# Other PSUM banks, earlier weight forms and an earlier silu table for the first up group, and another order of the last sums and scalings, in a hybrid encoder block

## The chip, the cores and the metric

The kernel runs on one core of a Trainium2 chip. The metric is the device time of one execution in microseconds (us). The core has five engines that work side by side: TensorE (PE in the profile; PEld is its weight load), VectorE (DVE), ScalarE (ACT), GpSimd (POOL) and SyncE (SP). Each runs its own instructions in the order in which they stand in the program and waits on semaphores for the others. SP, ACT and POOL also issue DMAs. Matmul results go to PSUM, which this kernel uses as eight banks of 128x512 floats.

## What is computed

One encoder layer over 512 tokens of width 2048: a gated mixer of two attentions, then a SwiGLU feed-forward, and a final RMS norm. What bears on the change:

```python
h2 = rms_norm(x, norm2_w[l]) * (1.0 + sc2) + sh2
ff = (jax.nn.silu(h2 @ w_ffn_gate[l]) * (h2 @ w_ffn_up[l])) @ w_ffn_down[l]
x = x + g2 * ff
...
return rms_norm(x, final_w)
```

The gate and up matrices are 2048 x 5632, the down matrix is 5632 x 2048, all float32.

## The kernel before, in words

**Split products.** Every float32 operand is split into a high part (rounded, written by ACT) and a low part (source minus high part, by DVE): `split`, lines 134 to 136. A product is three matmuls (`mm3`, lines 142 to 145): high by high, high by low, low by high. Of weights, the line-143 and line-144 matmuls read the high part and the line-145 matmul the low part.

**Seven products.** Most feed-forward products are 2x2 block products done with seven block products in place of eight (`group7`, lines 916 to 944), numbered r = 1 to 7 and run in the order `ORDER` = 1, 2, 3, 5, 6, 7, 4. The weights of one such product are made by `wforms` (lines 870 to 890) from two 512 KB loads `raw`: r = 1 takes a block of the first load as it is, r = 2 and 3 take the second load, r = 5 and 6 take the sums `ta`, r = 7 and 4 take the sums `tb`. Each of these four is split into a buffer `whl`, of which there are five in turn; `raw` also has five in turn, `ta` two, `tb` one. The token side has forms of its own: `xsums` makes sums `sa` and `sb`, `xforms` splits them into `x56`, `x3` and parts of the tiles `m`. The second call of `xsums` for the last quarter takes its `sb` out of the one `tb` buffer, the other call takes two `raw` buffers.

**The gate and up loop.** There are 11 column groups of 512 (`for n in range(FU)`, line 1008), each with a gate and an up product over four quarters `s` of the 2048 features, in the order 2, 3, 0, 1. One quarter of one product is 7 x 12 = 84 matmuls. The very first gate group is done classically, without the seven products, by `first_products` (lines 958 to 967), because it runs while the normed and transposed tokens are only arriving (`h2_part`, lines 804 to 814, which uses the banks S, S, T in turn). It holds the four banks `mm` to its end. Then four silu activations (line 1015) empty these banks, and the first up group starts through `group7`. Its results go to banks after the table `BANK` (line 845): r = 1, 2, 3, 5 to the four `mm` banks, 6 and 7 to the two S banks, 4 to Y. The bank T takes four dummy transposes (`stirred`, line 847) after the first quarter of the first up group. At the end of a group (lines 935 to 944) ACT and DVE add the banks up, and the next group takes the banks by the same table.

**The order of instructions.** A scheduler orders each engine's instructions from the program's order, the dependences and priorities; `tc.high_priority()` moves what stands in it forward, and `behind` (`keep_in_program_order`, line 285) keeps an instruction in its place.

**The end.** The last stage (lines 1285 to 1315) goes over four blocks of 128 tokens, `i` = 0 to 3. For each of four column groups `cc` PE does 12 matmuls, DVE multiplies the bank by the gate (`ro`, line 1280) and adds the residual (line 1281; the tiles are `xa` for columns 0 and 1, `xb`, `xd`), and ACT sums the squares (line 1282). For blocks 0 to 2, `row_rstd` then makes the reciprocal root (`rr`), four DVE instructions scale the block (line 1301) and four stores leave, half from SP and half from ACT. For block 3 the columns are multiplied by the final weights ahead of the root (line 1296), which only has to wait for the square; the root's sums stand in a high-priority part (lines 1305 to 1309), and then one column group is scaled by ACT and three by DVE; SP issues three of the four stores.

Of the kernel before, what the change touches and what calls it, by code (L numbers as in the profile page):

```python
# [32 lines left out]
EPS = 1e-6  # L33
# [56 lines left out]
def encoder_block(ctx: ExitStack, tc, xp, xT, c, ada1_w, ada2_w, b_ada, norm1_w, w_in, q_norm_w, k_norm_w, bias,  # L90
                  w_oa, w_ob, w_out, norm2_w, w_gate, w_up, w_down, final_w, rope, out):
    nc = tc.nc
    V, S, G = nc.vector, nc.scalar, nc.gpsimd

    const = ctx.enter_context(tc.tile_pool(name="const", bufs=1))
    small = ctx.enter_context(tc.tile_pool(name="small", bufs=4))
# [27 lines left out]
    def bank(tag):  # L124
        return ps.tile([P, 512], F32, tag=tag, name=tag, bufs={"mm": 4, "S": 2, "T": 1, "Y": 1}[tag])
# [120 lines left out]
    def row_rstd(acc):  # L246
        ssq = small.tile([P, 1], F32, tag="ssq", name="ssq")
        V.reduce_sum(ssq, acc, axis=AX.X)
        return rsqrt_mean(ssq, D, 1)
# [190 lines left out]
    r = token_rstd()  # L440
# [363 lines left out]
    def h2_part(s, a, t):  # L804
        tp = bank(next(turn))
        for q in range(2):
            for c in range(2):
                o = (2 * q + c) * P
                nc.tensor.transpose(tp[:, o:o + P], xn[s][:, 2 * t + c, (2 * a + q) * P:(2 * a + q + 1) * P], ident)
        for q in range(2):  # L810
            k = 4 * s + 2 * a + q
            S.activation(feature(s, a, t)[:, q], tp[:, q * 256:(q + 1) * 256].rearrange("p (c n) -> p c n", c=2),
                         AF.Identity, scale=s2[:, k:k + 1], bias=t2[:, k:k + 1])
        split(*(quarter(h, t) for h in mx[2 * s + a]), feature(s, a, t))
# [28 lines left out]
    LATE = (1, 5, 6, 7, 4, 2, 3)  # L843
    HALVES = (1,), (2, 3), (5, 6), (7, 4)
    BANK = {1: "mm", 2: "mm", 3: "mm", 5: "mm", 6: "S", 7: "S", 4: "Y"}

    def stirred(b):

        for o in range(0, 4 * P, P):
            last = behind(nc.tensor.transpose(b[:, o:o + P], ident, ident))  # L850
        stir_last.append(last.ins)
# [61 lines left out]
        d[3] = tuple(blk(h, 0) for h in x3)  # L913
        return d

    def group7(wsrc, xs, order, dst, stir=False):

        bk = {r: bank(BANK[r]) for r in ORDER}
        for n, s in enumerate(order):
            w = wsrc(s)  # L920
            if stir and n == 1:
                tp = bank("T")
                stirred(tp)
            for r in ORDER:
                (wh, wl), (xh, xl) = w[r], xs[s][r]
                for q in range(2):
                    for c in range(2):
                        o = bk[r][:, c * 256:(c + 1) * 256]
                        cs = slice(c * P, (c + 1) * P)
                        first, last = n == 0 and q == 0 and c == 0, n == len(order) - 1 and q == 1  # L930
                        with after_stir():
                            mm3(o, wh[:, q, cs], wl[:, q, cs], xh[:, q], xl[:, q], first, last, skip_group_check=True)
        p = {r: b.rearrange("p (c n) -> p c n", c=2) for r, b in bk.items()}
        (d11, d12), (d21, d22) = dst
        with tc.high_priority():
            p1 = io.tile([P, 512], F32, tag="io", name="p1").rearrange("p (c n) -> p c n", c=2)
            S.activation(p1, p[1], AF.Copy)
            V.tensor_add(d11, p[2], p1)
            V.tensor_add(d21, p[6], p1)
            V.tensor_add(d12, p[5], d21)  # L940
            V.tensor_add(d12, p[3], d12)
            V.tensor_add(d21, p[7], d21)
            V.tensor_add(d22, p[5], d21)
            V.tensor_sub(d21, d21, p[4])
# [31 lines left out]
    for s in (2, 3, 0, 1):  # L976
        for e in range(2):
            first_products(s, e, 1, False, (s, e) == (1, 1))
            if parts:
                h2_part(*parts.pop(0), 1)  # L980
        if s not in f_x:
            sums = {0: xsums(0, raw_tile("sa"), raw_tile("sb")), 1: xsums(1)}
            p_r.release()
            ca = form_pool("ca", "right")
            f_x.update({n: form_pool(f"f{n}", "right") for n in (0, 1)})
            c_p = form_pool("c", "right")
        hx[s] = xforms(f_x[s], s, *(sums[s] if s < 2 else xsums(s)))
# [20 lines left out]
    for n in range(FU):  # L1008
        cs = []
        for w in (w_gate, w_up):  # L1010
# [8 lines left out]
            def wsrc(s):  # L1019
                d = wforms(w, 4 * s, n * 512)  # L1020
                if s == 1 and n == FU - 1 and w is w_up:
                    first_pairs()
                return d
# [258 lines left out]
        S.activation(io.tile([P, 512], F32, tag="io", name="junk")[:, :n], to, AF.Square, accum_out=acc)  # L1282

    last_sq = small.tile([P, 2], F32, tag="ssq", name="last_sq")
    for i in range(NT):
        sl = slice(i * P, (i + 1) * P)
        for cc in range(4):
            final = i == NT - 1 and cc == 3
            for h in range(1 + final):
                b = bank("mm" if (i or cc > 1) and not h else "S")  # L1290
                hs = slice(h * 256, h * 256 + 256) if final else slice(0, 512)
                for k in range(4):
                    mm3(b[:, hs], xs[k][0][:, sl], xs[k][1][:, sl], *(t[:, hs] for t in wl[cc][k]), k == 0, k == 3)
                column(i, cc, b, hs.start, hs.stop - hs.start, last_sq[:, 0:1] if final and h else sq3[i][:, cc:cc + 1])
                if i == NT - 1:
                    V.tensor_mul(x2[cc][:, i, hs], x2[cc][:, i, hs], fw[:, cc * 512 + hs.start:cc * 512 + hs.stop])
        if i < NT - 1:
            r = row_rstd(sq3[i])
            for cc in range(4):
                cs = slice(cc * 512, (cc + 1) * 512)  # L1300
                V.scalar_tensor_tensor(x2[cc][:, i], x2[cc][:, i], r, fw[:, cs], op0=ALU.mult, op1=ALU.mult)
                (nc.scalar if cc % 2 else nc.sync).dma_start(out[i * P:(i + 1) * P, cs], x2[cc][:, i])
            continue
        with tc.high_priority():
            V.reduce_sum(last_sq[:, 1:2], sq3[i], axis=AX.X)
            V.tensor_scalar(last_sq[:, 1:2], last_sq[:, 1:2], 1.0 / D, EPS, op0=ALU.mult, op1=ALU.add)
            ms = small.tile([P, 24], F32, tag="ms", name="ms")[:, :1]
            V.scalar_tensor_tensor(ms, last_sq[:, 0:1], 1.0 / D, last_sq[:, 1:2], op0=ALU.mult, op1=ALU.add)
            r = inverse_root(ms)
        for cc in (1, 3, 0, 2):  # L1310
            if cc == 1:
                S.activation(x2[cc][:, i], x2[cc][:, i], AF.Copy, scale=r)
            else:
                V.tensor_scalar(x2[cc][:, i], x2[cc][:, i], r, None, op0=ALU.mult)
            (nc.scalar if cc == 1 else nc.sync).dma_start(out[i * P:(i + 1) * P, cc * 512:(cc + 1) * 512], x2[cc][:, i])
    p_s.release()
    p_e.release()
    wq.release()
# [27 lines left out]
```

## Time and profile before

| what | us |
|---|---|
| median of 3 runs | 2565.15 |
| lowest and highest of these | 2564.49 and 2567.37 |
| the profiled execution: its own time | 2564.97 |
| the profiled execution: its span, from the first to the last instruction | 2563.2 |
| PE busy in that span | 2525.6 |
| DVE, ACT busy | 1880.0, 1021.3 |

All times below are counted from the start of the profiled span. The first up group stands at about 1293 us, the last stage begins near 2508 us. A timeline row gives start, duration, engine, line, operation, output and inputs, their sizes, and in brackets how long the engine was idle before it and what ended that. The 1.8 us between span and own time lie outside the first and last instruction.

### The profile page before, as it was taken

How to read it: one execution, taken by the hardware profiler on the slowest of the kernel's cores; microseconds unless marked ns; L12 is line 12 of the kernel's file. 1: busy time of each engine (PE TensorE's matmuls, PEld its weight loads, DVE VectorE, ACT ScalarE, POOL GpSimd, SP SyncE). 2: the span in 40 equal slices, each digit the busy share in tenths (PEclk: the TensorE clock that was granted, in tenths of full speed). 3: DMA queues.
4: the chain of work that ended last, by engine and by line, in shares of the span. 5: the costliest groups of instructions: out<-in, count | busy, mean ns of one | idle time of the engine just before them, and what ended most of it. 6: DMA issues, size and time to landing. Idle time of an engine off the chain costs nothing.

```text
span 2563.2 us, 40435 instructions
## 1 busy us (share of the span) xinstructions
PE 2525.6 (99%) x16525; PEld 2281.8 (89%) x16525; DVE 1880.0 (73%) x2499; ACT 1021.3 (40%) x1407; POOL 151.3 (6%) x254
## 2 busy tenths in 40 slices
PE   7999999999999999999999999999999999999997
PEld 5888788888888788888999999999999998999996
DVE  8984776456566567555798888888888885687877
ACT  5223544223333332225754444444444454434333
POOL 0000000111011111011000000000000000000010
PEclk8999999999999999999999999999999999999999
DMA  9864234855655877676444444433444456546562
GB/s 342 309 237 146 69 99 145 257 183 180 187 172 188 294 239 247 205 266 211 132 132 130 128 125 132 129 119 116 132 124 124 132 171 219 199 139 235 185 253 106
DMA packets 217466, 457.46 MB, mean 178 GB/s; under 512 B 15056, under 2 KB 68672, under 8 KB 208832
## 3 DMA queue, kind: packets, MB, share of 16 engines
q1 hardware_dynamic: 179872, 308.19, 37.5%
q0 software_dynamic: 29728, 132.20, 15.1%
q10 hardware_dynamic: 7680, 14.48, 1.6%
q8 instruction: 130, 2.13, 0.3%
q14 instruction: 56, 0.46, 0.1%
HBM read 410.74 MB, written 44.07 MB: 177 GB/s over the span
## 4 chain that ended last, share of the span: by engine, by line
PE 91%; DVE 4%; DMA 2%; ACT 1%; issue 1%; SPq 0%; DVEq 0%; ACTq 0%
PE mm L145 19%; PE mm L144 19%; PE mm L143 19%; PE S L143 7%; PE S L145 7%; PE S L144 7%; PE Y L143 3%; PE Y L144 3%; PE Y L145 3%; PE T L145 1%; PE T L144 1%; PE T L143 1%; DMA yr<-y 1%; DMA raw<-in_w_down 1%; DVE raw L414 1%
## 5 line engine op out<-in xcount | busy, mean ns | idle before, releaser
L135 ACT ACTIVATE whl<-raw 128x1024 fp32r<-128x1024 f32 (+1 forms) x483 | 464.3, 962 | 836.4 <-PE mm L145 381.5
L136 DVE TENSOR_TENSOR whl<-raw,whl 128x1024 fp32r<-128x1024 f32 (+1 forms) x483 | 531.6, 1110 | 315.9 <-ACT whl L135 315.4
L136 DVE TENSOR_TENSOR whl<-ta,whl 128x1024 fp32r<-128x1024 f32 x104 | 127.4, 1225 | 74.4 <-ACT whl L135 73.0
L135 ACT ACTIVATE whl<-tb 128x1024 fp32r<-128x1024 f32 x104 | 110.8, 1065 | 153.0 <-PE S L145 129.0
L135 ACT ACTIVATE whl<-ta 128x1024 fp32r<-128x1024 f32 x104 | 110.4, 1062 | 149.0 <-PE mm L145 104.7
L313 DVE SCALAR_TENSOR_TENSOR acc<-mw,cact,acc 128x1024 f32<-128x1024 f32 x124 | 158.5, 1278 | 14.0 <-DMA mw<-in_ada_w 13.8
L136 DVE TENSOR_TENSOR whl<-tb,whl 128x1024 fp32r<-128x1024 f32 x104 | 127.1, 1223 | 9.0 <-ACT whl L135 6.0
L291 POOL DMA_DIRECT2D mw<-in_ada_w x112 | 59.8, 534 | 713.6 <-DVE acc L313 422.0
L143 PE MATMUL S<-x56h,whl 128*128 128x256 f32 x336 | 92.8, 276 | 0.4 <-ACT whl L135 0.4
L144 PE MATMUL S<-x56l,whl 128*128 128x256 f32 x336 | 92.7, 276 | 0.0
L143 PE MATMUL mm<-x3h,whl 128*128 128x256 f32 x336 | 92.7, 276 | 0.0
L144 PE MATMUL mm<-x3l,whl 128*128 128x256 f32 x336 | 92.7, 276 | 0.0
L145 PE MATMUL mm<-x3h,whl 128*128 128x256 f32 x336 | 92.7, 276 | 0.0
L143 PE MATMUL mm<-x56h,whl 128*128 128x256 f32 x336 | 92.7, 276 | 0.0
L144 PE MATMUL mm<-x56l,whl 128*128 128x256 f32 x336 | 92.7, 276 | 0.0
L145 PE MATMUL mm<-x56h,whl 128*128 128x256 f32 x336 | 92.7, 276 | 0.0
L145 PE MATMUL S<-x56h,whl 128*128 128x256 f32 x336 | 92.7, 276 | 0.0
L881 DVE TENSOR_TENSOR ta<-raw,ta 128x512 f32<-128x512 f32 x104 | 71.7, 689 | 27.2 <-DMA raw<-in_w_down 25.0
L880 DVE TENSOR_TENSOR ta<-raw 128x512 f32<-128x512 f32 x104 | 71.9, 691 | 26.8 <-DMA raw<-in_w_down 24.6
L143 PE MATMUL mm<-whl,s 128*128 128x256 f32 x320 | 88.5, 276 | 0.0
L144 PE MATMUL mm<-whl,s 128*128 128x256 f32 x320 | 88.4, 276 | 0.0
L145 PE MATMUL mm<-whl,s 128*128 128x256 f32 x320 | 88.4, 276 | 0.0
(1530 smaller groups left out, 8544.4 us busy)
## 6 DMA issues: line engine op xcount, KB each, us to landing
raw<-in_w_in SPq DMA_DIRECT2D x133, 512.0 KB, 4.0
mw<-in_ada_w POOLq DMA_DIRECT2D x112, 512.0 KB, 4.8
raw<-in_w_gate SPq DMA_DIRECT2D x92, 512.0 KB, 3.9
raw<-in_w_up SPq DMA_DIRECT2D x88, 512.0 KB, 3.8
raw<-in_w_down SPq DMA_DIRECT2D x88, 512.0 KB, 5.0
raw<-in_ada_w POOLq DMA_DIRECT2D x29, 1024.0 KB, 6.5
raw<-in_w_out SPq DMA_DIRECT2D x48, 512.0 KB, 4.7
ffd<-c SPq DMA_DIRECT2D x10, 1024.0 KB, 4.7
```

The lines of the kernel that those rows point to most:

```text
L135: pin(S.activation(hi, src, AF.Copy))
L136: pin(eng.tensor_sub(lo, src, hi))
L143: nc.tensor.matmul(o, lh, rh, start=start, stop=False, **kw)
L144: nc.tensor.matmul(o, lh, rl, start=False, stop=False, **kw)
L145: nc.tensor.matmul(o, ll, rh, start=False, stop=stop, **kw)
L291: mod["queue"].dma_start(w, ada2_w[n * P:(n + 1) * P, :])
L313: behind(V.scalar_tensor_tensor(acc, part, cact[:, k:k + 1], acc, op0=ALU.mult, op1=ALU.add))
L414: V.scalar_tensor_tensor(raw, raw, 1.0, call, op0=ALU.mult, op1=ALU.mult, accum_out=y)
L880: V.tensor_sub(t1, b12, b11)
L881: V.tensor_sub(t2_, b22, t1)
```

## The change

Three things, in the functions shown above. First, the first up group gets a table of its own, `FIRST`: r = 1 and 2 go to the S banks, 3 to Y, 5 to T, and 6, 7, 4 to three of the four `mm` banks; the fourth (`spare_bank`) takes the dummy transposes. Its first weight forms stand in a high-priority part. Second, a silu of one element is put behind the last `h2_part`. Third, block 2's four scalings and stores are moved behind block 3's columns, between the steps of block 3's root, which lose their high priority; the fourth of block 3's scalings goes from DVE to ACT, and its store from SP to ACT.

```diff
+    FIRST = {1: "S", 2: "S", 3: "Y", 5: "T", 6: "mm", 7: "mm", 4: "mm"}
...
-        bk = {r: bank(BANK[r]) for r in ORDER}
+        spare_bank = bank("mm") if first_group else None
+        bk = {r: bank((FIRST if first_group else BANK)[r]) for r in ORDER}
         for n, s in enumerate(order):
-            w = wsrc(s)
-            if stir and n == 1:
-                tp = bank("T")
-                stirred(tp)
+            with tc.high_priority() if first_group and n == 0 else contextlib.nullcontext():
+                w = wsrc(s)
+            if first_group and n == 1:
+                stirred(spare_bank)
...
                 h2_part(*parts.pop(0), 1)
+                if not parts:
+                    dummy = small.tile([P, 1], F32, tag="ssq", name="silu")
+                    behind(S.activation(dummy, ones[:, 0:1], AF.Silu))
...
+    def finish(i, cc, r, pin=lambda ins: ins):
+        cs = slice(cc * 512, (cc + 1) * 512)
+        pin(V.scalar_tensor_tensor(x2[cc][:, i], x2[cc][:, i], r, fw[:, cs], op0=ALU.mult, op1=ALU.mult))
+        (nc.scalar if cc % 2 else nc.sync).dma_start(out[i * P:(i + 1) * P, cs], x2[cc][:, i])
...
-        if i < NT - 1:
+        if i < NT - 2:
             r = row_rstd(sq3[i])
             for cc in range(4):
...
+                finish(i, cc, r)
+        elif i == NT - 2:
+            r = row_rstd(sq3[i])
+    behind(V.reduce_sum(last_sq[:, 1:2], sq3[i], axis=AX.X))
+    behind(V.tensor_scalar(last_sq[:, 1:2], last_sq[:, 1:2], 1.0 / D, EPS, op0=ALU.mult, op1=ALU.add))
+    for cc in range(2):
+        finish(i - 1, cc, r, behind)
+    ms = small.tile([P, 24], F32, tag="ms", name="ms")[:, :1]
+    behind(V.scalar_tensor_tensor(ms, last_sq[:, 0:1], 1.0 / D, last_sq[:, 1:2], op0=ALU.mult, op1=ALU.add))
+    finish(i - 1, 2, r, behind)
+    r_last = inverse_root(ms)
+    finish(i - 1, 3, r, behind)
+    for cc in (1, 3, 0, 2):
+        if cc % 2:
+            S.activation(x2[cc][:, i], x2[cc][:, i], AF.Copy, scale=r_last)
+        else:
+            V.tensor_scalar(x2[cc][:, i], x2[cc][:, i], r_last, None, op0=ALU.mult)
+        (nc.scalar if cc % 2 else nc.sync).dma_start(out[i * P:(i + 1) * P, cc * 512:(cc + 1) * 512], x2[cc][:, i])
```

Between these two places, and on POOL throughout, all instructions stand in the order of before. On SP one load for the next gate group went ahead of the first up group's eighth load, and the last stores moved as the diff says. What moved is shown at three places; in the rows of after, line numbers are those of the changed file (`split` keeps lines 135 and 136; line 881 of before is 882 in after and so on).

**ACT at the start of the first up group.** `whl<-raw`, `whl<-ta` and `whl<-tb` are the high parts of weight forms, `x56h`, `x3h`, `m0h` and `m2h` of token forms; `c<-mm` are the four silus that empty the gate group's banks. Before:

```order
L135 ACTIVATE x56h<-sa 128x1024
L135 ACTIVATE x3h<-sb 128x512
L135 ACTIVATE x56h<-sa 128x1024
L135 ACTIVATE x3h<-sb 128x512
L135 ACTIVATE m2h<-sb 128x512
L135 ACTIVATE whl<-ta 128x1024
L1015 ACT_TABLE_LOAD
L1015 ACTIVATE c<-mm 128x2x256 x4
L135 ACTIVATE whl<-tb 128x1024
L135 ACTIVATE whl<-raw 128x512
L135 ACTIVATE whl<-raw 128x1024
```

Now:

```order
L985 ACT_TABLE_LOAD
L985 ACTIVATE silu<-ones 128x1
L135 ACTIVATE m0h<-sb 128x512
L135 ACTIVATE whl<-raw 128x1024
L135 ACTIVATE whl<-ta 128x1024
L135 ACTIVATE x56h<-sa 128x1024
L135 ACTIVATE x3h<-sb 128x512
L135 ACTIVATE x56h<-sa 128x1024
L135 ACTIVATE x3h<-sb 128x512
L135 ACTIVATE m2h<-sb 128x512
L1020 ACTIVATE c<-mm 128x2x256 x4
L135 ACTIVATE whl<-raw 128x1024
```

The table load stands ahead of `m0h`, `whl<-ta` ahead of the token forms, and the second quarter's `whl<-raw` ahead of the first quarter's `whl<-tb`, which is the next row of after.

**DVE at the same place.** The rows are the low parts of the same forms and the sums `ta` and `tb`. Before:

```order
L136 TENSOR_TENSOR whl<-raw,whl 128x512
L136 TENSOR_TENSOR x56l<-sa,x56h 128x1024
L136 TENSOR_TENSOR x3l<-sb,x3h 128x512
L136 TENSOR_TENSOR x56l<-sa,x56h 128x1024
L136 TENSOR_TENSOR x3l<-sb,x3h 128x512
L136 TENSOR_TENSOR m2l<-sb,m2h 128x512
L136 TENSOR_TENSOR whl<-raw,whl 128x1024
L882 TENSOR_TENSOR tb<-raw 128x512
L883 TENSOR_TENSOR tb<-ta,raw 128x512
L136 TENSOR_TENSOR whl<-ta,whl 128x1024
L880 TENSOR_TENSOR ta<-raw 128x512
L136 TENSOR_TENSOR whl<-tb,whl 128x1024
```

Now:

```order
L136 TENSOR_TENSOR whl<-ta,whl 128x1024
L136 TENSOR_TENSOR m0l<-sb,m0h 128x512
L136 TENSOR_TENSOR x56l<-sa,x56h 128x1024
L136 TENSOR_TENSOR x3l<-sb,x3h 128x512
L136 TENSOR_TENSOR x56l<-sa,x56h 128x1024
L136 TENSOR_TENSOR x3l<-sb,x3h 128x512
L136 TENSOR_TENSOR m2l<-sb,m2h 128x512
L883 TENSOR_TENSOR tb<-raw 128x512
L884 TENSOR_TENSOR tb<-ta,raw 128x512
L136 TENSOR_TENSOR whl<-raw,whl 128x1024
L881 TENSOR_TENSOR ta<-raw 128x512
L136 TENSOR_TENSOR whl<-tb,whl 128x1024
```

The first quarter's `whl<-raw` and `whl<-ta` went ahead of the token forms; between the second `tb` and the low part of `whl<-tb` there now stand the second quarter's `whl<-raw` and its `ta<-raw`, which reads a load of its own.

**DVE in the last block.** `rr` is the reciprocal root, `gf` holds the gate factors and the final weights. Before, from the root of block 2 on:

```order
L239 SCALAR_TENSOR_TENSOR rr<-rt,rr 128x1
L1301 SCALAR_TENSOR_TENSOR xa<-xa,rr,gf 128x512 x2
L1301 SCALAR_TENSOR_TENSOR xb<-xb,rr,gf 128x512
L1301 SCALAR_TENSOR_TENSOR xd<-xd,rr,gf 128x512
L1296 TENSOR_TENSOR xa<-xa,gf 128x512
L1280 TENSOR_TENSOR ro<-mm,gf 128x512
L1281 TENSOR_TENSOR xa<-xa,ro 128x512
L1280 TENSOR_TENSOR ro<-mm,gf 128x512
L1296 TENSOR_TENSOR xa<-xa,gf 128x512
L1281 TENSOR_TENSOR xb<-xb,ro 128x512
```

Now the last rows, from the last column's multiplication on:

```order
L1307 TENSOR_TENSOR xd<-xd,gf 128x256
L1314 TENSOR_REDUCE last_sq<-sq_22260 128x1
L1315 TENSOR_SCALAR last_sq<-last_sq 128x1
L1293 SCALAR_TENSOR_TENSOR xa<-xa,rr,gf 128x512 x2
L1319 SCALAR_TENSOR_TENSOR ms<-last_sq 128x1
L1293 SCALAR_TENSOR_TENSOR xb<-xb,rr,gf 128x512
L236 RECIPROCAL rr<-rt 128x1
L237 SCALAR_TENSOR_TENSOR rt<-rr 128x1
L238 TENSOR_TENSOR rt<-rt,ms 128x1
L239 SCALAR_TENSOR_TENSOR rr<-rt,rr 128x1
L1293 SCALAR_TENSOR_TENSOR xd<-xd,rr,gf 128x512
L1327 TENSOR_SCALAR xa<-xa,rr 128x512
```

The four scalings of block 2 (line 1301, now 1293) left the place behind their root and stand between the steps of block 3's root. In the part between, `xa<-xa,gf` of the second column (line 1296, now 1307) went one row ahead, in front of the third column's `ro`, and the last `xd<-xd,gf` now stands ahead of the sums of the root instead of behind them.

More of the change, by code (lines that the diff above doesn't have):

```diff
@@ L914, in xforms, with group7 @@
         return d
-    def group7(wsrc, xs, order, dst, stir=False):
-        bk = {r: bank(BANK[r]) for r in ORDER}
+    def group7(wsrc, xs, order, dst, first_group=False):
+        spare_bank = bank("mm") if first_group else None
+        bk = {r: bank((FIRST if first_group else BANK)[r]) for r in ORDER}
         for n, s in enumerate(order):
-            w = wsrc(s)
-            if stir and n == 1:
-                tp = bank("T")
-                stirred(tp)
+            with tc.high_priority() if first_group and n == 0 else contextlib.nullcontext():
+                w = wsrc(s)
+            if first_group and n == 1:
+                stirred(spare_bank)
             for r in ORDER:
@@ L1296, in encoder_block @@
                     V.tensor_mul(x2[cc][:, i, hs], x2[cc][:, i, hs], fw[:, cc * 512 + hs.start:cc * 512 + hs.stop])
-        if i < NT - 1:
+        if i < NT - 2:
             r = row_rstd(sq3[i])
             for cc in range(4):
[L1300 to L1315, printed above, removed]
+                finish(i, cc, r)
[16 more added lines that the diff above has]
+        (nc.scalar if cc % 2 else nc.sync).dma_start(out[i * P:(i + 1) * P, cc * 512:(cc + 1) * 512], x2[cc][:, i])
     p_s.release()
```

## The prediction

> **What bounds the kernel now.** I read the page first: its busy line and its chain of waits.
>
> ```profile
> PE 2525.6 (99%) x16525; PEld 2281.8 (89%) x16525; DVE 1880.0 (73%) x2499; ACT 1021.3 (40%) x1407; POOL 151.3 (6%) x254
> ...
> PE 91%; DVE 4%; DMA 2%; ACT 1%; issue 1%; SPq 0%; DVEq 0%; ACTq 0%
> ```
>
> PE is busy for 2525.6 of the span's 2563.2 us, so all its idle time is 37.6 us. The change leaves the number of matmuls alone; it can win only where PE waits or runs slow, and behind the last matmul. So the next views are PE's timeline round the first up group, and three windows (length, PE, PEld, DVE, ACT and POOL busy, granted clock, DMA share, GB/s).
>
> ```profile
> 1293.30 0.28 PE L145 MATMUL mm<-m3h,whl 128*128 128x256 f32 x1
> 1294.01 0.39 PE L143 MATMUL S<-x56h,whl 128*128 128x256 f32 x1 [0.44 <-ACT whl L135]
> ...
> 1295.92 0.58 PE L143 MATMUL mm<-m4h,whl 128*128 128x256 f32 x1 [1.41 <-ACT c L1015]
> ...
> 1299.08 0.35 PE L145 MATMUL mm<-m5h,whl 128*128 128x256 f32 x1
> ...
> 1306.89 0.60 PE L850 MATMUL T<-ident 128*128 128x128 f32 x4
> 1307.24 0.37 PE L143 MATMUL mm<-m6h,whl 128*128 128x256 f32 x1
> ...
> 1335.90 0.28 PE L143 MATMUL mm<-m4h,whl 128*128 128x256 f32 x1
> ...
> 1339.98 0.28 PE L143 MATMUL mm<-x56h,whl 128*128 128x256 f32 x1
> ...
> 845.20:848.70 3.50, 2.06 (x8) 1.16 (x7) 2.43 (x3) 1.94 (x4) 1.22 (x3) 1.00 0.69 199
> ...
> 1292.40:1295.81 3.41, 1.68 (x13) 1.27 (x11) 3.41 (x5) 3.38 (x6) 0.00 (x0) 1.00 0.87 268
> 1295.81:1299.23 3.42, 3.31 (x15) 3.31 (x16) 3.42 (x6) 3.33 (x7) 0.00 (x0) 0.50 0.60 187
> ```
>
> The reader sees the first up group start badly: two waits (0.44 for a weight form, 1.41 for the silu `c` that empties a bank), then 3.42 us at half clock. From 1335.90 to 1339.98 lie three products r of 12 matmuls, so one takes 1.36 us, 0.113 a matmul. Without loss the group would begin at 1293.41, its first quarter last 7 x 1.36 = 9.52, the dummy transposes 0.35 (1306.89 to 1307.24), and the second quarter begin at 1303.28. It begins at 1307.24: the place costs **3.96 us**. Of that some 1.6 are the half clock (15 matmuls, 14 spacings, took 3.16 us from 1295.92 to 1299.08 in place of 1.58), the rest are the waits. The end is the other place; the digits are the tenths of DMA time in 40 slices from 2557 to 2563.2.
>
> ```profile
> 2549.76 0.28 PE L145 MATMUL S<-w,fl 128*128 128x256 f32 x1
> ...
> 2545.53 0.19 ACT L1282 ACTIVATION_READ_ACCUMULATOR junk<-xa 128x1 f32 x1
> ...
> 2545.39 1.42 DVE L1301 SCALAR_TENSOR_TENSOR xa<-xa,rr,gf 128x512 f32<-128x512 f32 x2
> ...
> 2548.05 0.69 DVE L1296 TENSOR_TENSOR xa<-xa,gf 128x512 f32<-128x512 f32 x1
> 2548.65 0.69 DVE L1280 TENSOR_TENSOR ro<-mm,gf 128x512 f32<-128x512 f32 x1
> 2549.37 0.69 DVE L1281 TENSOR_TENSOR xa<-xa,ro 128x512 f32<-128x512 f32 x1
> 2549.98 0.68 DVE L1280 TENSOR_TENSOR ro<-mm,gf 128x512 f32<-128x512 f32 x1
> 2550.91 0.69 DVE L1296 TENSOR_TENSOR xa<-xa,gf 128x512 f32<-128x512 f32 x1 [0.25 <-ACT junk L1282]
> ...
> 2554.46 0.42 DVE L1281 TENSOR_TENSOR xd<-xd,ro 128x256 f32<-128x256 f32 x1
> 2555.51 0.16 DVE L1308 SCALAR_TENSOR_TENSOR ms<-last_sq 128x1 f32<-128x1 f32 x1 [0.63 <-ACT junk L1282]
> ...
> 2557.52 0.48 DVE L1314 TENSOR_SCALAR xb<-xb,rr 128x512 f32<-128x512 f32 x1
> ...
> 2557.23 0.33 SPq L1315 DMA_DIRECT2D out<-xd  x1
> ...
> 2558.14 0.47 SPq L1315 DMA_DIRECT2D out<-xb  x1
> ...
> DMA  0000001899999999999999997733000000000000
> ```
>
> PE is done at 2550.04; from there DVE is last, then the stores. The four stores of block 3 keep the DMA engines busy from about 2558.0 to 2561.3, 0.8 us each; the first data moved 0.8 after its issue at 2557.23.
>
> **The change part by part.** *Banks.* Products 1, 2, 3 and 5 now write banks that the gate group does not hold, so the wait for `c` goes: when r = 6 wants a `mm` bank, at 1293.41 + 4 x 1.36 = 1298.85, the silus are done, since the gate group ends at 1293.58 and they take 2.06.
>
> ```profile
> 1288.49 1.07 ACT L135 ACTIVATE whl<-raw 128x1024 fp32r<-128x1024 f32 x1 [2.25 <-DMA raw<-in_w_up]
> ...
> 1293.98 1.28 ACT L1015 ACT_TABLE_LOAD   x1
> 1295.27 2.06 ACT L1015 ACTIVATE c<-mm 128x512 f32<-128x512 f32 x4
> 1297.27 1.06 ACT L135 ACTIVATE whl<-tb 128x1024 fp32r<-128x1024 f32 x1
> ```
>
> *Table load.* 1.28 us and a silu of one element fall into ACT's 2.25 us of waiting for a load ahead of 1288.49, and so cost nothing; without that cover, at most some 1.5.
>
> *What is late next:* the weights of r = 7. PE wants their low part with its third matmul, at 1293.41 + 5 x 1.36 + 2 x 0.113 = 1300.44.
>
> ```profile
> 1291.86 0.70 DVE L136 TENSOR_TENSOR x3l<-sb,x3h 128x512 fp32r<-128x512 f32 x1
> ...
> 1294.80 1.23 DVE L136 TENSOR_TENSOR whl<-raw,whl 128x1024 fp32r<-128x1024 f32 x1
> 1295.94 0.69 DVE L882 TENSOR_TENSOR tb<-raw 128x512 f32<-128x512 f32 x1
> 1296.54 0.70 DVE L883 TENSOR_TENSOR tb<-ta,raw 128x512 f32<-128x512 f32 x1
> ...
> raw<-in_w_up SPq DMA_DIRECT2D x1, 512.0 KB, 4.7
> ```
>
> `tb` has one buffer, which the last `sb` holds until `m2l`, so the early weight forms stop short of it. Ahead of the first `tb` DVE has the rows of before and `whl<-ta` besides; such a row of 1024 columns keeps the next from starting for 1.14 (1294.80 to 1295.94), one of 512 for 0.60. So the second `tb` ends at 1297.24 + 1.14 = 1298.38, and ACT splits it from 1298.5 to 1299.55. DVE meanwhile does the second quarter's `whl<-raw` (1298.28 to 1299.42, counted to the next start) and meets `ta<-raw`, which reads a load that SP issues only when `x3l` is done. `x3l` now has `whl<-raw` and `whl<-ta` ahead of it, 2 x 1.14: done 1294.84 instead of 1292.56. The load issued there took 4.7 us, so it lands near 1299.6. Queued behind `ta<-raw` on DVE is `whl<-tb`: it starts 0.60 later, at 1300.2, and ends at 1301.43. PE waits **1.0 us** at r = 7, of which 0.8 would be there by DVE's queue alone. The second quarter then begins at 1304.3 instead of 1307.24: **-2.9** (-3.1 to -2.0). Its first weights are ready at 1300.2 + 1.14 + 3 x 0.60 + 0.69 = 1303.83, just ahead of PE. The load that SP now issues one place later belongs to the last quarter, at 1304.3 + 2 x 9.52 = 1323: nothing.
>
> *Handover.* The next group wants the four `mm` banks in the order 1, 2, 3, 5, and the bank for its r = 5 is now that of the first group's r = 4, the one that DVE reads last.
>
> ```profile
> 1339.57 0.68 DVE L944 TENSOR_TENSOR c<-c,Y 128x512 f32<-128x512 f32 x1
> ```
>
> That ends at 1340.25, PE wants r = 5 at 1339.98: **+0.3** (0 to 0.6). The dummy transposes keep their place in PE's stream.
>
> *Tail.* The four scalings (2545.39 to 2548.05, 2.66 us) leave DVE's queue there, but then the squares hold DVE up. `xa<-xa,gf` of the second column may start 1.54 after its sum (2549.37 to 2550.91); the `ro` that filled this gap now stands behind it. With these distances (0.60 for 512 columns, 0.72 to a row that needs the one ahead, 1.54 over a square, 0.34 to 0.46 by the same pattern for 256): the first `xa` starts at 2545.75, when its square is done; the second column's sum at 2547.06, its `xa` at 2548.60; the third's sum at 2549.93; the last sum of `xd` at 2552.75. Its square holds the next row for 1.05 (2554.46 to 2555.51): 2553.80. Two small sums end at 2554.4, two scalings take 1.33, and `ms` comes at 2555.74, 0.23 *later* than before. The scalings of `xb` and `xd` and the root's steps bring the last `xb` to 2558.2 instead of 2557.52. DVE ends 0.7 later: one scaling of 0.48 went to ACT, and more waits came in. The stores are worse, since eight instead of four leave behind 2555. Three go ahead of 2558, but block 2's `xd` is issued at 2557.9 and block 3's four follow within 0.9 us. Five stores at 0.8, with data from 2558.8, end at 2562.8 instead of 2561.3: **+1.5**. Bounds: +0.5 if only the later issue counts (2558.65 against 2558.14), +1.9 if the store of block 2's `xd` also waits for ACT's second scaling, which stands ahead of it on ACT.
>
> Sum against the profiled execution: 2564.97 - 2.9 + 0.3 + 1.5 = **2563.9**. That execution lies 0.2 under the median, so I take the sum as it stands.
>
> On the slow window, row and rule differ. The Trainium skill (TensorE: Matmul & The Clock Gate, Part 1) puts the fall to half clock behind at least one idle window of about 3.4 us; here one with 1.73 of its 3.41 us idle was enough, and the measurement decides. By that rule the two waits alone would go and the half clock would not have been theirs: 2565.5.
>
> **The rivals.** (a) *The half clock was an accident of that execution.* The window with 1.73 us of idle time was followed by half clock, that at 845.2 with 1.44 of 3.50 was not. Before's two waits lie 2.3 us apart from end to end, so whether enough of both falls into one window depends on where its edge lies. Executions in which it did not had 1.6 less to lose: 2565.5. Against it: the profiled execution is no slower than the median. The Trainium skill's same page calls these windows free-running, so their edges would differ from run to run.
>
> (b) *Slower: the wait at r = 7 brings the half clock back.* If the load behind `ta<-raw` takes as long as the longest one there,
>
> ```profile
> DMA to landing us min/median/max: 3.6/3.7/5.6
> ```
>
> it lands 0.9 later, PE waits 1.9 us in one stretch, and 1.6 come on top: -3.96 + 1.9 + 1.6 + 0.3 + 1.5 = +1.3, 2566.3. It decides between 1.44 and 1.73 us of idle time in a window. Against it: this load has one neighbour only.
>
> (c) *The tail is neutral*: the stores keep up, and DVE's filling makes up for the squares: 2564.97 - 2.9 + 0.3 = 2562.4. For it: 2.66 us did leave the place behind block 2's root. Against it: the row of nines in the DMA digits.
>
> That the change does not do what it says is ruled out for the banks: the order shows them.
>
> **How the numbers follow.** Forecast 0.55, (a) 0.20, (b) 0.08, (c) 0.17. The cases span 2562.4 to 2566.3; with no wait at r = 7 and a neutral tail it would be 2561.4, and runs of before lay up to 2.2 over their median. I give 2561.5 to 2566.8. A measurement of this kernel can tell about 0.2% (5.1 us) from no change: under 2560.0 or over 2570.3. No case reaches either; I leave 0.04 for each.
>
> **What would show it.** In the profile after: no wait of PE for a silu and no half clock near 1296; one wait of about 1.0 us of an L145 matmul on `mm` for DVE `whl` near 1300.4, and the dummy transposes near 1304; a wait of 0.3 at the next group's r = 5; DVE waiting for `junk` in four places at the end, and DMA busy until about 1.5 us later after the last matmul than before. The forecast is wrong if that last distance grows by less than 0.5, or if PE waits over 1.5 us at r = 7.

## The result, and the profile after

| | runs | median us | lowest to highest |
|---|---|---|---|
| before | 20 | 2564.51 | 2559.96 to 2571.23 |
| changed | 20 | 2592.57 | 2562.05 to 2598.33 |
| changed, lower group | 5 | 2562.63 | 2562.05 to 2563.92 |
| changed, upper group | 15 | 2594.99 | 2589.74 to 2598.33 |

The ratio of the times is 1.0086 with a 95% interval of 1.0066 to 1.0107: the change makes the kernel slower, by some 0.9%. No run of the changed kernel lies between 2563.92 and 2589.74. The forecast of 2563.9 is met by one run in four; three in four lie 30 us above it, and no rival foresaw them. The profiled execution (2563.92 us, span 2562.1) belongs to the lower group, so it shows what the change did at the two places, and nothing of the 30 us.

The busy line of its page, then PE's timeline at the first up group and at the next group's r = 5:

```profile
PE 2523.9 (99%) x16525; PEld 2280.1 (89%) x16525; DVE 1879.4 (73%) x2498; ACT 1021.6 (40%) x1409; POOL 151.9 (6%) x254
```

```profile
1292.91 0.28 PE L143 MATMUL S<-m4h,whl 128*128 128x256 f32 x1
...
1300.92 0.38 PE L145 MATMUL mm<-m4h,whl 128*128 128x256 f32 x1 [0.81 <-DVE whl L136]
...
1303.54 0.60 PE L851 MATMUL mm<-ident 128*128 128x128 f32 x4
1303.89 0.37 PE L143 MATMUL S<-m6h,whl 128*128 128x256 f32 x1
...
1336.51 0.28 PE L145 MATMUL mm<-x3h,whl 128*128 128x256 f32 x1
1337.03 0.36 PE L143 MATMUL mm<-x56h,whl 128*128 128x256 f32 x1 [0.24 <-DVE c L946]
```

The reader sees the group begin at 1292.91 without a wait, one wait of 0.81 at r = 7 for DVE's low part, the second quarter at 1303.89, and a wait of 0.24 at the handover. The first quarter with its transposes takes 10.98 instead of 13.83 us (1293.41 to 1307.24 before). The granted clock (last column but two) stays at 1.00, and a stretch of 30 us holds 267 or 268 matmuls, whether ahead of or behind the handover:

```profile
1296.00:1304.00 8.00, 7.18 (x64) 6.99 (x63) 7.96 (x12) 4.45 (x6) 0.00 (x0) 1.00 0.71 241
1304.00:1334.00 30.00, 30.00 (x267) 30.00 (x266) 26.79 (x35) 12.41 (x14) 0.00 (x0) 1.00 0.44 140
1340.00:1370.00 30.00, 30.00 (x268) 30.00 (x267) 24.80 (x30) 13.05 (x14) 0.00 (x0) 1.00 0.55 176
1700.00:1800.00 100.00, 100.00 (x885) 100.00 (x884) 86.23 (x107) 42.92 (x47) 0.00 (x0) 1.00 0.40 120
```

The end: the last matmul, DVE's timeline, and the DMA digits of 2556 to 2562.1:

```profile
2546.90 0.28 PE L145 MATMUL S<-w,fl 128*128 128x256 f32 x1
```

```profile
2543.39 0.69 DVE L1307 TENSOR_TENSOR xa<-xa,gf 128x512 f32<-128x512 f32 x1 [0.39 <-ACT junk L1287]
...
2546.26 0.69 DVE L1307 TENSOR_TENSOR xa<-xa,gf 128x512 f32<-128x512 f32 x1 [0.85 <-ACT junk L1287]
...
2551.45 0.42 DVE L1307 TENSOR_TENSOR xd<-xd,gf 128x256 f32<-128x256 f32 x1 [0.63 <-ACT junk L1287]
...
2553.37 0.15 DVE L1319 SCALAR_TENSOR_TENSOR ms<-last_sq 128x1 f32<-128x1 f32 x1
...
2555.83 0.48 DVE L1327 TENSOR_SCALAR xb<-xb,rr 128x512 f32<-128x512 f32 x1
```

```profile
DMA  2039999999999999999999999631000000000000
```

Counted from PE's end (2547.18 here, 2550.04 before), `ms` comes at 6.2 instead of 5.5, DVE ends at 9.1 instead of 8.0, and the DMA engines fall still at about 13.1 (28 slices of 0.15 behind 2556) instead of 11.3. Three waits of DVE for a square stand there where four were expected. Not all of these differences come from the new order of the end; the part on the end below separates them.

### The profile page after: what moved, and what is told of

The parts are those of the page before. It is cut to its first block, busy times and chain, and to the rows that moved or that the text cites. A ratio compares the mean times of both kernels' runs of the same rounds, so it can differ in the third digit from the quotient of the medians.

```text
span 2562.1 us, 40438 instructions
## 1 busy us (share of the span) xinstructions
PE 2523.9 (99%) x16525; PEld 2280.1 (89%) x16525; DVE 1879.4 (73%) x2498; ACT 1021.6 (40%) x1409; POOL 151.9 (6%) x254
## 4 chain that ended last, share of the span: by engine, by line
PE 90%; DVE 5%; DMA 2%; ACT 1%; issue 1%; DVEq 0%; ACTq 0%
PE mm L145 18%; PE mm L143 18%; PE mm L144 18%; PE S L143 7%; PE S L145 7%; PE S L144 7%; PE Y L143 3%; PE Y L144 3%; PE Y L145 3%; PE T L145 1%; PE T L144 1%; PE T L143 1%; DMA yr<-y 1%; DVE whl L136 1%; DVE raw L414 1%
## 5 line engine op out<-in xcount | busy, mean ns | idle before, releaser
L313 DVE SCALAR_TENSOR_TENSOR acc<-mw,cact,acc 128x1024 f32<-128x1024 f32 x124 | 158.4, 1277 | 13.0 <-DMA mw<-in_ada_w 12.9
L143 PE MATMUL mm<-x3h,whl 128*128 128x256 f32 x320 | 88.3, 276 | 0.0
L145 PE MATMUL mm<-x3h,whl 128*128 128x256 f32 x320 | 88.3, 276 | 0.0
L143 PE MATMUL S<-x56h,whl 128*128 128x256 f32 x320 | 88.3, 276 | 0.0
L145 PE MATMUL S<-x56h,whl 128*128 128x256 f32 x320 | 88.3, 276 | 0.0
```

The costliest lines, as they stand in the source:

```text
L143: nc.tensor.matmul(o, lh, rh, start=start, stop=False, **kw)
L145: nc.tensor.matmul(o, ll, rh, start=False, stop=stop, **kw)
L313: behind(V.scalar_tensor_tensor(acc, part, cact[:, k:k + 1], acc, op0=ALU.mult, op1=ALU.add))
```

## The experiments

First, the changed kernel was taken apart into its two places.

**The changed kernel again (twice).** Edit: none.

> The changed kernel once more, unaltered. Of its 20 runs 5 lay at 2562.1 to 2563.9 us, as forecast, and 15 at 2589.7 to 2598.3; the profiled one is of the lower group and shows nothing of the other. All theories expect the two groups again, about 30 us apart and about three in four above. What is wanted is a profile of the upper group. Theory F (first group): the extra 30 us begin at the first up group near 1293 us and not before. Theory T (tail): they lie behind the last matmul. Theory L (layout): they lie somewhere that the change did not touch, ahead of 1280 us.

Measured: 12 runs, 5 from 2561.38 to 2566.49, 7 from 2591.90 to 2596.57; the profiled one (2561.38) in the lower group. With the second,

> The changed kernel unaltered once more, for a profile of the upper group, which about 7 in 10 of its runs belong to. If the profile shows it, the 30 us are a stretch in which PE runs slower or waits longer than in the lower group; theory W expects it behind 1293 us.

which gave one run of 2564.44, the changed kernel stands at 22 upper runs of 33. No profile of the changed kernel's upper group exists: all three of its profiles fell in the lower one. The kernel before, run beside it, had 3 of 29 runs at 2593 to 2604: the upper group is not new, only rare there.

**The first up group alone, and the end alone.** Edit of the first: `finish` and the last stage as in the kernel before; of the second: `FIRST`, `spare_bank`, the high priority and the dummy silu taken out.

> Only the first up group's part (table of banks, early weight forms, early silu table); the end as before. By the terms of the prediction the lower group lies at 2564.5 - 2.9 + 0.3 = 2562, as low as 2560. Theory F: most runs still lie 30 us higher, near 2591. Theory T: no run does. Theory L: either.

Measured: 8 of 12 runs in the lower group with a median of 2561.54, 4 in the upper with 2593.3. So theory T falls; theory F has the right part of the change, though it put most runs into the upper group. The lower median is 2.6 under that of the 119 lower runs of before in all batches (2564.09), and 3.4 under that of the 26 beside it (2564.91).

> Only the new order of the end; the first up group as before. By the terms of the prediction the lower group lies 1.5 us above before, at 2566. Theory T: most runs lie 30 us higher, near 2595. Theory F: none does. Theory L: either.

Measured: none of 11 runs in the upper group, median 2565.58, ratio 0.9999 [0.999, 1.0007]. The end brings no 30 us. Its forecast cost of 1.5 can't be told from nothing by these times: the 26 lower runs of before beside it have a median of 2564.91.

Then the first group's part was taken apart.

```diff
-                    behind(S.activation(dummy, ones[:, 0:1], AF.Silu))
+                    behind(S.activation(dummy, ones[:, 0:1], AF.Copy))
```

> The changed kernel with the one-element silu turned into a one-element copy, so that the silu table is loaded at the first silu again, some 1.3 us on ACT near 1295 us. Theory W (PE that no longer rests here lets the upper group in): only the time and place of PE's rest changes, the upper group stays frequent unless a rest of 2 us or more comes back near 1300. Theory D (the early table load itself brings the 30 us): no run in the upper group. Theory L (where instructions lie in memory): the count of instructions stays, so the upper group stays at about 6 in 10.

Measured: 4 of 12 runs upper (2592.24 to 2603.31), 7 lower (median 2565.6), and one of 3168.8 at a mean granted clock of 0.75, which no profile shows. Theory D falls. PE's waits in the profile are 1.6 for weights and 0.2 at the handover.

Edit: only the dummy silu added to the kernel before.

> The kernel before with the early one-element silu alone; banks, weight forms and end as before. Theory D: the upper group is frequent, 4 in 10 or more. Theory W: rare, as in the kernel before (3 of 49 so far), if PE still rests over 1.5 us near 1294; PE's rest there should be shorter by up to 1.28. Theory L: as often as in the first-group-only kernel (4 of 12), since ACT gets the same two instructions more.

Measured: none of 10 runs upper, median 2561.4 (an eleventh took 10580.96 at a mean granted clock of 0.60, again without a profile); ratio 0.9992 [0.9981, 1.0002]. One wait of PE is left of the two, and no half clock came:

```profile
1291.29 0.28 PE L145 MATMUL mm<-m3h,whl 128*128 128x256 f32 x1
1292.46 0.38 PE L143 MATMUL mm<-m4h,whl 128*128 128x256 f32 x1 [0.89 <-ACT c L1018]
```

Theory D falls again, and theory L with it: the program has the same one ACT instruction more as the first part alone (x1408 on both pages, x1407 before), which had 4 upper runs of 12.

Edit: only `FIRST` and `spare_bank` added to the kernel before.

> The kernel before with the new table of banks alone; the weight forms keep their old place and the silu table is loaded at the first silu. Theory W: frequent upper group only if PE's rest near 1293 is gone; the late weight forms should leave a rest of some 1 to 2 us, so few. Theory D and theory L: as rare as before.

Measured: 6 of 12 runs upper. Theory W expected few, since PE's rest is still there (0.90 for a weight form), and falls too. The profiled run, 2596.09, is of the upper group, and shows the 30 us. Its busy line, PE's timeline at the handover, and windows ahead of and behind it:

```profile
PE 2556.4 (99%) x16525; PEld 2312.0 (89%) x16525; DVE 1882.1 (73%) x2499; ACT 1022.3 (39%) x1407; POOL 151.9 (6%) x254
```

```profile
1340.75 0.28 PE L145 MATMUL mm<-x3h,whl 128*128 128x256 f32 x1
1341.27 0.35 PE L143 MATMUL mm<-x56h,whl 128*128 128x256 f32 x1 [0.25 <-DVE c L946]
...
2219.76 0.28 PE L145 MATMUL mm<-whl,s 128*128 128x256 f32 x1
2219.89 0.60 PE L852 MATMUL T<-ident 128*128 128x128 f32 x4
```

```profile
1310.00:1335.00 25.00, 25.00 (x223) 25.00 (x223) 21.56 (x28) 10.48 (x12) 0.00 (x0) 1.00 0.48 144
1345.00:1375.00 30.00, 30.00 (x257) 30.00 (x256) 23.71 (x30) 12.28 (x14) 0.00 (x0) 1.00 0.52 164
1700.00:1800.00 100.00, 100.00 (x852) 100.00 (x851) 80.48 (x99) 41.80 (x45) 0.00 (x0) 1.00 0.41 126
...
2230.00:2260.00 30.00, 30.00 (x267) 30.00 (x266) 24.49 (x32) 11.23 (x13) 1.08 (x2) 1.00 0.39 129
```

PE is not idle for 30 us more; it is busy for 32.5 more than in the changed kernel's profile. Behind the wait of 0.25 a stretch of 30 us holds 257 matmuls, not 267, and one of 100 us 852, not 885, at a granted clock of 1.00 and with nothing to wait for. By the starts in the trace the distance is 117.8 ns instead of 113.3 from 1341.27 on, to the end of the gate and up loop near 2128. The first down products, to 2215.6, are 512 wide; behind them 36 matmuls of 256 columns still run at 117.8, and only behind the four dummy transposes at 2219.89 is it 113.3 again. The 6684 matmuls of the stretch in the loop by 4.44 ns are 29.7 us; most of the other 2.8 lies near 848.6, where this execution has some 7 us of half clock and the changed kernel's profile none. I call these the slow and the quick pace. Neither is the half clock: the granted clock is 1.00 in both.

The groups of the two pages (the changed kernel's, then this one's) say the same by their mean: 276 and 281 ns.

```profile
L143 PE MATMUL S<-x56h,whl 128*128 128x256 f32 x320 | 88.3, 276 | 0.0
```

```profile
L143 PE MATMUL S<-x56h,whl 128*128 128x256 f32 x320 | 89.9, 281 | 0.0
```

So the handover's wait, which the change brought in, is suspected. Four kernels test it.

```diff
+            if second and n == 1:
+                stirred(bank("T"))
```

> The changed kernel with four more dummy transposes (bank T) after the first quarter of the second gate group, so behind the short wait at the handover. The profile of the banks-only kernel shows the upper group: from that wait on (1341 us) each matmul takes 117.8 ns instead of 113.3, to the end of the gate and up loop. Theory P (the short wait leaves PE in a slower pace, which lasts until a matmul of another form comes): the pace lasts 50 matmuls at most, 0.2 us, so no run in the upper group; all near 2563. Theory S (the slower pace comes from something that stands over the whole loop, such as banks, ports or loads, and the wait only happens to lie at its start): upper group as often as in the changed kernel, 7 in 10.

Measured: 7 of 12 runs upper. The profiled one, 2597.7, is one of them. Theory P, which had no upper run, falls: the handover's wait of 0.24 left the quick pace here, and the four transposes that were to end the slow pace began it. The count is that of theory S, but the profile is not: the loop runs at the quick pace up to the transposes, so no cause that stands over the whole loop sets it alone.

```profile
1338.50:1343.50 5.00, 5.00 (x46) 5.00 (x45) 5.00 (x6) 1.41 (x2) 0.00 (x0) 1.00 0.56 206
1345.00:1375.00 30.00, 30.00 (x257) 30.00 (x256) 23.54 (x30) 11.94 (x13) 0.00 (x0) 1.00 0.42 130
```

The first window lies between the wait and the transposes (46 in 5 us: the quick pace; at the slow one it would be 44 or 45), the second behind them.

```diff
+    SECOND = {**BANK, 5: "T"}
```

> The changed kernel with r = 5 of the second gate group in bank T instead of the fourth mm bank, so that the wait of 0.24 us at the handover goes and nothing else moves. Theory P: no run in the upper group, the median 0.24 under the changed kernel's lower group, near 2562.5; the wait of some 1 us at r = 7 stays and is ended by the dummy transposes behind it. Theory S: upper group as often as in the changed kernel.

Measured: 1 of 11 runs upper (2595.83), where theory S had seven in ten and theory P none; of the others the median is 2563.24. The profiled run, 2571.18, had no wait at the handover, one of 2.4 us at r = 7, and two of 1.0 and 0.9 in the down products, behind which the slow pace held for 190 us.

```diff
+    SECOND = {**BANK, 5: "Y", 4: "T"}
```

> The kernel before, nothing of the change in it, with r = 5 of the second gate group in bank Y (and r = 4 in T), so that it takes the bank that the first up group's last sum reads, and PE waits there some 0.25 us. Theory P: upper group in 3 to 7 of 10 runs, 30 us above the rest. Theory S: upper group as rare as in the kernel before (3 of 78 runs so far), time within 0.3 us of it.

Measured: 5 of 12 runs upper (2593.18 to 2598.62), against 2 of the 35 of before beside it. The profiled run (2566.39) is of the lower group; it shows the wait, with the quick pace behind it:

```profile
1341.73 0.36 PE L143 MATMUL Y<-x56h,whl 128*128 128x256 f32 x1 [0.24 <-DVE c L945]
...
1345.00:1375.00 30.00, 30.00 (x267) 30.00 (x266) 24.80 (x31) 12.85 (x14) 0.00 (x0) 1.00 0.54 172
```

This is the kernel before with two banks of one group exchanged and a wait of 0.24 by it: that is enough for an upper group. That the wait counts and not the bank is shown by the other runs: the slow pace came with r = 5 in `mm` (the banks alone) and in Y (below), and both banks were seen with the quick one.

> The change of the first up group, with r = 5 of the second gate group in bank T as in the run without the handover, and the end as before. By theory P and the terms of the prediction: no upper group, and 2564.8 - 2.9 - 1.5 x 0 = 2562 or a little under, 1.5 under the same kernel with the new end. Theory S: upper group in 3 to 7 of 10 runs.

Measured: none of 11 upper; median 2563.22, ratio 0.9997 [0.9986, 1.0008]. With this, theory S has failed in three kernels. The time misses what was expected, though: it is 0.9 under the 119 lower runs of before, not 2.6, and equal to that of the same kernel with the new end (2563.24 for its ten lower runs), not 1.5 under it.

What was open then is how a break in PE's stream sets the pace. Three kernels made from the one before put the breaks elsewhere.

Edit: the call of `stirred` taken out.

> The kernel before without its four dummy transposes, which stand behind the first quarter of the first up group (it leaves out no part of the result). Theory P2 (every break in PE's stream, a wait or a few matmuls of another form, draws the pace anew, and it stays until the next break; the odds of the slow pace are about a half behind a wait, and small behind these transposes): the last break ahead of the long stretch is now the wait of 1.41 us, so 3 to 7 of 10 runs lie 30 us higher. Theory P3 (only the short wait at the handover, in the middle of the loop's steady supply, draws the slow pace): no more runs in the upper group than before, 5 of 113 so far; time 0.35 lower.

Measured: 5 of 6 runs at 2591.82 to 2597.53, one at 2565.80. Now the half clock behind the wait for the silu is the last break, and the profiled run (2593.64) has the slow pace from the moment that the clock is back:

```profile
1293.72 0.48 PE L143 MATMUL mm<-m4h,whl 128*128 128x256 f32 x1 [1.41 <-ACT c L1012]
```

```profile
1293.90:1297.30 3.40, 3.40 (x17) 3.40 (x18) 3.40 (x6) 3.38 (x6) 0.00 (x0) 0.50 0.57 167
1300.00:1330.00 30.00, 30.00 (x257) 30.00 (x257) 23.90 (x29) 12.53 (x14) 0.00 (x0) 1.00 0.42 124
1700.00:1800.00 100.00, 100.00 (x851) 100.00 (x850) 80.72 (x100) 40.99 (x44) 0.00 (x0) 1.00 0.39 118
```

So the four dummy transposes of the kernel before, which look useless, hold its upper group down to 5 of 124 runs. Theory P3 falls.

Edit: every group behind the first takes `BANK` with r = 5 and r = 4 in Y and T by turns.

> The kernel before with r = 5 and r = 4 in Y and T by turns, so that r = 5 of each of the 20 groups behind the first up group takes the bank that the group ahead reads last, and PE waits some 0.25 us at each handover: 5 us of waits in all. Theory P2 and P3: each wait draws anew, so one profile holds 20 draws, about half of them slow; the time is 2564 + 5 + about 15 with a spread of some 4 us, and no two groups. A theory by which the first draw holds for the whole stretch: two groups again, at 2569 and 2599.

Measured: four runs of 2581.59 to 2588.18 (a fifth of 4169.99 at a mean granted clock of 0.57, without a profile), no two groups. Windows in six groups one behind the other:

```profile
1380.00:1410.00 30.00, 30.00 (x267) 30.00 (x267) 24.06 (x30) 12.12 (x14) 0.00 (x0) 1.00 0.39 115
1418.00:1448.00 30.00, 30.00 (x257) 30.00 (x257) 23.70 (x29) 12.25 (x14) 0.00 (x0) 1.00 0.53 163
1455.00:1485.00 30.00, 30.00 (x267) 30.00 (x266) 22.81 (x27) 13.52 (x15) 0.00 (x0) 1.00 0.45 126
1496.00:1526.00 30.00, 30.00 (x257) 30.00 (x256) 23.71 (x30) 12.25 (x14) 0.00 (x0) 1.00 0.53 166
1535.00:1565.00 30.00, 30.00 (x267) 30.00 (x266) 23.90 (x29) 13.05 (x14) 0.00 (x0) 1.00 0.44 131
1575.00:1605.00 30.00, 30.00 (x258) 30.00 (x257) 23.71 (x30) 11.93 (x13) 0.00 (x0) 1.00 0.51 155
```

From the third handover on, quick and slow groups take turns to the end. In a slow group PE comes later to the bank and waits little (145 or 146 ns from start to start, not 118); that small break, always at bank T, ends the slow pace each time. The slow groups all have r = 5 in Y; the first group with Y ran quick, so the bank alone doesn't set the pace. So each break sets the pace anew, for the stretch to the next one, but not as a coin does. For the waits at a handover, all profiles together, the distance from the last start ahead of the wait to the first behind it (taken from the records, which are finer than the rows) goes with what follows:

| distance, ns | waits | slow behind |
|---|---|---|
| 515 to 517 | 7 | 0 |
| 519 to 523 | 12 | 10 |

The two quick ones among the longer differ in the next distance (195 ns, not 192 to 194). So at the handovers a few ns of the restart go with what follows; nine of the ten slow ones, though, are of this one kernel. Elsewhere the distance doesn't tell: in the profile of the end alone a wait of 517 ns among the down products was followed by the slow pace,

```profile
2389.57 0.39 PE L144 MATMUL S<-whl,s 128*128 128x256 f32 x1 [0.24 <-DVE whl L136]
...
2391.00:2420.00 29.00, 29.00 (x249) 29.00 (x248) 24.09 (x28) 10.20 (x11) 2.91 (x5) 1.00 0.72 265
```

and two waits there of 1261 ns each were followed by different paces (slow in the kernel without the handover, quick in the next one).

Edit: `stirred(bank("T"))` behind the first quarter of every group.

> The kernel before with the four dummy transposes behind the first quarter of every group, not only of the first: 20 times 0.35 = 7 us more. It shows what a draw by transposes gives, 21 times in one profile. Theory P2 with small odds behind the transposes: nearly all stretches at 113.3 ns, 2564.5 + 7 = 2571.5, none of the runs 20 us higher. If the transposes draw like the waits: about half of the stretches at 117.8, 2571 + 15 = 2586. If they pass from one pace to the other each time: the paces alternate from group to group.

Measured: 2580.66 to 2582.72, all five. Windows in six groups in a row:

```profile
1345.00:1375.00 30.00, 30.00 (x267) 30.00 (x266) 25.54 (x33) 13.03 (x14) 0.00 (x0) 1.00 0.37 107
1382.00:1412.00 30.00, 30.00 (x257) 30.00 (x256) 23.05 (x29) 12.17 (x14) 0.00 (x0) 1.00 0.36 105
1422.00:1452.00 30.00, 30.00 (x267) 30.00 (x266) 24.34 (x32) 12.20 (x14) 0.00 (x0) 1.00 0.38 113
1462.00:1492.00 30.00, 30.00 (x267) 30.00 (x266) 24.03 (x31) 13.02 (x14) 0.00 (x0) 1.00 0.35 105
1500.00:1530.00 30.00, 30.00 (x257) 30.00 (x257) 23.96 (x31) 11.94 (x13) 0.00 (x0) 1.00 0.37 108
1540.00:1570.00 30.00, 30.00 (x267) 30.00 (x266) 23.94 (x31) 12.46 (x14) 0.00 (x0) 1.00 0.34 104
```

Every third stretch is slow, seven in all to the end of the loop: the transposes set the pace too, again by a rule and not by chance. None of my three guesses names this pattern.

## Why the prediction was wrong, point by point

**The step that failed** is the handover: "That ends at 1340.25, PE wants r = 5 at 1339.98: +0.3 (0 to 0.6)". The wait is there and as long as said, 0.24. What failed is that it was priced by its own length alone. The prediction put what follows at nothing: PE restarts at one of two paces, and keeps it for the 6684 matmuls to the end of the loop. The kernels without a wait at the handover, and with the first group's transposes as the last break, had the upper group in 6 of 167 runs (before 5 of 124; the end alone 0 of 11, the table alone 0 of 10, without the handover 1 of 11 and, with the old end, 0 of 11); those with it and no break behind it in 41 of 80 (the changed kernel 22 of 33, the first part alone 4 of 12, with the copy 4 of 11, the banks alone 6 of 12, the wait added to the kernel before 5 of 12). So the term is 0.24 + 29.7 in about two of three runs of the changed kernel. Its own upper group has no profile; that it is this pace follows from the banks alone, whose profile shows it behind the same wait, and from the runs that took the wait out or put it in.

It could have been read from the trace of before. Its first gate group ran at the slow pace until transposes came, and at the quick one behind them, at the same granted clock:

```profile
1249.00:1259.00 10.00, 10.00 (x87) 10.00 (x86) 7.52 (x21) 7.22 (x12) 0.00 (x0) 1.00 0.38 100
1261.00:1271.00 10.00, 10.00 (x91) 10.00 (x90) 6.53 (x9) 6.85 (x13) 0.00 (x0) 1.00 0.16 51
```

```profile
1259.84 0.60 PE L809 MATMUL T<-ident,x 128*128 128x128 f32 x4
```

All sixteen profiles show the slow pace there, behind matmuls of 512 columns, and the quick one behind the transposes. I took 0.1133 for the one distance of a matmul at full clock, and did not ask what the dummy transposes are for.

On this the Trainium skill (TensorE: Matmul & The Clock Gate, Part 1) gives a back-to-back distance at full clock, the columns over 2.4 GHz and some 2.5 ns, an estimate of 109 ns for 256 columns. The trace, in which each matmul has a weight load of its own, does not agree: 113.3 and 117.8 were measured at a granted clock of 1.00, and which of the two holds is set at a restart.

**The first quarter**: forecast -2.9, measured 10.98 against 13.83, -2.85. The wait at r = 7 came as described (DVE's `whl` behind `ta<-raw`), 0.81 instead of 1.0; in the profiles of the other kernels with this first group it took 0.8 to 2.4.

**The end**: forecast +1.5 with bounds of 0.5 and 1.9; DMA ended 13.1 behind PE instead of 11.3, +1.8. Of this, 0.5 is not the new order's: DVE came to block 3 later against PE. Its first `ro` of that block, here and before, is

```profile
2541.13 0.68 DVE L1285 TENSOR_TENSOR ro<-mm,gf 128x512 f32<-128x512 f32 x1
```

```profile
2543.49 0.68 DVE L1280 TENSOR_TENSOR ro<-mm,gf 128x512 f32<-128x512 f32 x1
```

From its start to the end of the span it is 21.0 here and 19.7 before, +1.3. All sixteen profiles agree: 19.7 in the nine with the old end, 21.0 to 21.2 in the seven with the new. Counted from PE's end the two overlap (12.8 to 13.7 and 12.9 to 15.0). From that `ro` on, `ms` comes 0.22 later (forecast 0.23) and DVE ends 0.67 later (0.7), so the mechanism holds, with five stores in a row from 2556.3 to 2560.3, 0.8 each. Rival (c), a neutral end, falls by the profiles. The times alone don't show it: the lower runs of the changed kernel (11, median 2563.29) lie 1.75 above those of the first part alone (2561.54), but the two kernels without the handover stand at the same time with the new end as with the old (2563.24 and 2563.22).

**The sum** for the lower group, 2563.9, is met: 2563.92 by the profiled run, 2563.29 by the median of 11. That it fits to 0.02 is luck: the three terms came to -1.3 (-2.85, +0.24, +1.3) instead of -1.1, and three differences outside them add up to +0.25: PE came to the first up group 0.5 earlier than before, lost some 0.25 of that further on, and DVE was the 0.5 later.

**Rival (a)**, the half clock as an accident, was half right. The two waits of before's first group stand in six profiles of kernels that keep them; three had the half clock behind them (before, the end alone, without the transposes), three not (the wait added, and the two with breaks in every group). The Trainium skill's same page calls the windows free-running, and these six profiles agree: the same two waits (0.35 to 0.49, and 1.41) gave both outcomes. Near 847 us, which no change here touches, the half clock came in four of the sixteen profiles. **Rival (b)**, a half clock behind r = 7, was not seen, not even behind 2.4 us of waiting, so the idle time of 1.44 to 1.73 on which it was to turn does not decide alone. I had looked for the slower case in the clock alone.

**What wins.** The early silu table alone, one instruction more than before, has a median of 2561.4 beside 2564.4 and no upper run in 10; its interval of the ratio, 0.9981 to 1.0002, still holds no change. The new banks show no more gain than that in the times, and bring the handover.

**Left open**: what inside PE makes the two paces, what decides between them at a break, and why the changed kernel met the slow one in 22 of 33 runs where its relatives with the same wait met it in 19 of 47.

## What to carry to other kernels

Price a wait of PE not by its own length alone, but by the stretch that follows until the next break: here 0.24 us of idle time decided over 30 us. Count matmuls per window at full clock in the trace that there is; two counts for one shape mean two paces, and an instruction that seems to do nothing may be what sets the better one. Look at all times of a kernel, not at one profiled execution: a median between or above two groups says that the profile shows one of them.

## What the runs showed of the hardware

In the long stretches matmuls of 256 columns in float32 run back to back at 113.3 or at 117.8 ns (267 or 257 in 30 us), both at a granted clock of 1.00. (The last 24 of the program, whose moving operand is `fl`, stand at 119.7 in all sixteen profiles; nothing here says why.) The pace lasts for as long as matmuls of this form follow without a break, over 6600 of them in three profiles. It was seen to change behind a wait, behind the return from half clock, and behind four transposes, and was the slow one behind matmuls of 512 columns at the first gate group and behind the first down products, in all sixteen profiles. At the handovers the distance over the wait went with it (519 to 523 against 515 to 517 ns); behind equal transposes in every group every third stretch was slow.
